# Hybrid encoder trunk: activations spread over the next products, the first pair's weight operands by way of DRAM, and a fixed TensorE order around the output projection

## The chip, the cores and the metric

The kernel runs on one core of a Trainium2 chip: TensorE (PE) multiplies, VectorE (DVE), ScalarE (ACT) and GpSimd (POOL) do the elementwise work, SyncE (SP) and the other engines' queues issue transfers (DMA) between device memory (DRAM) and the on-chip memory; products accumulate in banks of PSUM. The metric is the device time of one execution in microseconds, median of the runs.

## The reference

One layer of a Hymba-like encoder over two inputs, x_prompt (1, 256, 1024) and x_sample (1, 1024, 1024), all in float32, so 1280 tokens in all, ten tiles of 128:

```python
def encoder_layer(x, ...):
    h = rmsnorm(x, attn_norm_g)
    proj = h @ w_in
    a = mla_group(...)
    b = na_group(...)
    mix = jnp.concatenate([rmsnorm(a, mla_out_g), rmsnorm(b, na_out_g)], axis=-1)
    x = x + mix @ w_o
    h2 = rmsnorm(x, ffn_norm_g)
    x = x + (jax.nn.silu(h2 @ w_gate) * (h2 @ w_up)) @ w_down
    return x
```

and a last rmsnorm. `a` is latent attention, `b` neighbourhood attention, 512 columns each. D_MODEL is 1024, the FFN is 2816 wide (22 blocks of 128, taken as 11 pairs). The change touches what begins with `x + mix @ w_o` and ends ahead of `@ w_down`.

## The kernel before

**Split products.** Each float32 operand is split into a high part (a cast to fp32r, made on ACT or POOL) and a low part (the operand less its high part, made on DVE or POOL). A product is three matmuls, high by high, high by low, low by high (`mm3`, L108 to L112).

**Output projection.** The ten tiles t run one after the other. `mix_in` (L868) loads a tile of attention output `m`, squares it on ACT (L878), gets `rm`, the reciprocal root, on POOL (`rstd_of`, L89 and L91) and scales on POOL (L882). `mix_T` (L887) turns it by 8 transposes into `trm` and splits it (ACT L99, DVE L100) into `mT`. `out_proj` (L902) has 16 products of 128x512 in two banks `po`; DVE adds them to the residual `x` (L913). `ffn_in` (L918) squares x on ACT (L922), gets `rh` on POOL, scales on DVE (L925) to h2, turns it by 8 more transposes `trh` (L937), and evicts them with the gain (DVE L941, ACT L947) into X[k, j]: four blocks k of 256 features by three blocks j of 428 tokens (the last 424 used).

**Gate and up projections.** Each pair of feature blocks is multiplied by a fast bilinear scheme: 20 products of sums of weight blocks (weight operands `wr`) by sums of X (`S[n]`, n = 1 to 20), added up in PSUM chains and evicted into `C` (first use by ACT L1113, later ones added by DVE L1111). A product is 6 matmuls of 128x428 (`product`, L1097). For pair fp = 0, gate G and up U are multiplied together, 240 matmuls in the order `SEQ0`. After that come 20 phases of 120 matmuls in the order `SEQ`: for each pair 1 to 10 first gate (i = 0), then up (i = 1); the last phase has `SEQ0` again. The S operands are sums on DVE (`sums`, L965) and splits (`put_S`, ACT L958, DVE L959); some are made under the output projection, the rest under the first pair (`build_S`). Weight operands are sums on POOL (`sum_w`, L998), a cast on ACT (L990) and a low part on POOL or DVE (L992), in a ring of 3 slots at the first pair and 4 later. The raw weights come by SP, 1 MB for each phase.

**Activation.** `gate` is SiLU on ACT (L1129). `activate` (L1131) multiplies U by G in four blocks on DVE (L1132) and makes the sums which the down projection wants (L1138). Each result is stored to DRAM (`act_d`) by a DMA that ACT issues (`store`, L67):

```python
            if i == 1 and not last_one:
                if at == 10:
                    activate(G, C, "22", fp)
                elif at == 15:
                    activate(G, C, "12", fp)
```

The blocks "11" and "21" follow behind the up phase's last product, and fall in the next gate phase.

**Order.** SP's instructions run as written. On the other engines a scheduler sets the order when the program is built, from its own costs; `issue_after` holds a piece behind another instruction. Each engine then runs its instructions strictly in that order, and one that waits holds up all behind it.

Of the kernel before, what the change touches and what calls it, by code (L numbers as in the profile page):

```python
# [2 lines left out]

# [15 lines left out]
P = 128  # L19
# [20 lines left out]
def encoder_trunk(ctx: ExitStack, tc: tile.TileContext, x_tm, x_T, g_attn, w_c, w_v, w_qk,  # L40
# [794 lines left out]
    SE = rS.tile([P, 10 * 2 * XC], F32R, name="SE").rearrange("p (n s c t) -> p n s c t", n=5,  # L835
# [11 lines left out]
    rw, rt0, rm, rt1, rxm = r3 = [pool(nm) for nm in ("r3w", "r3t0", "r3m", "r3t1", "r3x")]  # L847
# [20 lines left out]
    def mix_in(t):  # L868
# [4 lines left out]
        mn = rm.tile([P, D], F32, name="m", bufs=3)  # L873
        ss = rm.tile([P, 2], F32, name="ssm", bufs=2)
        r = rm.tile([P, 2], F32, name="rm", bufs=2)
        for i in range(2):
            hs = slice(i * 512, (i + 1) * 512)
            nc.scalar.activation(mn[:, hs], mx[:, hs], AF.Square, accum_out=ss[:, i:i + 1])  # L878
        rstd_of(r, ss, 512)
        for i in range(2):  # L880
            hs = slice(i * 512, (i + 1) * 512)
            mixed[0] = nc.gpsimd.tensor_scalar(out=mn[:, hs], in0=mx[:, hs],  # L882
                                               scalar1=r[:, i:i + 1], scalar2=1.0,
                                               op0=ALU.mult, op1=ALU.mult).ins
        return mn

    def mix_T(t, mn):  # L887
        mT = (rt1 if t % 2 else rt0).tile([P, 2, KC, P], F32R, name=f"mT{t % 2}")
        for q in range(2):
# [4 lines left out]
            last_split[0] = split_ps(mT[:, 0, 4 * q:4 * q + 4], mT[:, 1, 4 * q:4 * q + 4], tr)  # L894
        return mT
# [6 lines left out]
    def out_proj(t, mT, x):  # L902
        added = []
        for hf in range(2):
            hs = slice(hf * 512, (hf + 1) * 512)
            ps = po.tile([P, 512], F32, name="po", bufs=2)
            with ExitStack() as es:
                if t == 0 and hf:
                    es.enter_context(tc.issue_after(last_os[0]))
                for kc in range(KC):  # L910
                    last = mm3(ps, mT[:, 0, kc], mT[:, 1, kc], wo[kc][:, 0, hs],
                               wo[kc][:, 1, hs], kc == 0, kc == KC - 1)
            added.append(nc.vector.tensor_add(out=x[:, hs], in0=ps, in1=x[:, hs]).ins)  # L913
        return last, added

    normed = [None]

    def ffn_in(t, x):  # L918
# [6 lines left out]
        done_ = [nc.vector.tensor_scalar(out=h2, in0=x, scalar1=r, scalar2=1.0, op0=ALU.mult,  # L925
                                         op1=ALU.mult).ins]
# [6 lines left out]
        for q in range(2):  # L933
            tr = po.tile([P, 4, P], F32, name="trm" if t >= NT - 2 and q else "trh", bufs=1)
            for i in range(4):
                kc = 4 * q + i
                nc.tensor.transpose(tr[:, i], h2[:, kc * P:(kc + 1) * P], ident)  # L937
            for j, to, of in cuts:
                if q == 0:
                    for k in range(2):  # L940
                        ev = nc.vector.tensor_mul(  # L941
                            out=X[k, j][:, :, to], in0=tr[:, 2 * k:2 * k + 2, of],
                            in1=gf[:, 2 * k:2 * k + 2].unsqueeze(2).to_broadcast(
                                [P, 2, of.stop - of.start]))
# [4 lines left out]
        return done_ + [ev.ins]  # L949

    def put_S(n, raw_, negate=False):
# [5 lines left out]
        else:  # L957
            nc.scalar.copy(out=h, in_=raw_)  # L958
            nc.vector.tensor_sub(out=l, in0=raw_, in1=h)  # L959

    ADD, SUB = ALU.add, ALU.subtract

    def sums(eng, cs, *steps):
        for o, a, op, b in steps:
            eng.tensor_tensor(out=X[o][:, :, cs], in0=X[a][:, :, cs], in1=X[b][:, :, cs], op=op)  # L965
# [7 lines left out]
    def put_(n, at):  # L973
# [6 lines left out]
              put_(17, (2, 1)), add_((3, 0), (3, 1), SUB, (3, 0)), add_("14", (2, 1), ADD, (1, 1)),  # L980
              add_((0, 1), (0, 1), SUB, (3, 0)), add_((1, 1), (1, 1), SUB, (3, 0)))

    LAST_SUMS = {16: (("16", (2, 1), ADD, (1, 2)),), 15: (((1, 0), (1, 2), SUB, (1, 0)),),
                 1: (((2, 0), (1, 2), SUB, (2, 0)), ((2, 0), (2, 0), SUB, (2, 2)),
                     ((2, 2), (2, 2), SUB, "16")),
                 20: (((1, 2), (3, 2), SUB, (1, 0)),),
                 12: (((3, 2), (2, 0), ADD, (3, 2)),), 19: (((3, 1), (2, 0), ADD, (3, 1)),)}
# [20 lines left out]
    cur = mix_T(0, mix_in(0))  # L1008
    load(gf, g_ffn)
    def B(k, i=slice(0, 2)):  # L1010
        return raw[:, i, k]

    LATER = {4: FIRST[0:4], 5: FIRST[4:], 7: SECOND[0:4], 8: SECOND[4:]}
    for t in range(NT):
        with ExitStack() as es:
            if t:
                es.enter_context(tc.issue_after(last_split[0]))
            nxt = mix_T(t + 1, mix_in(t + 1)) if t + 1 < NT else None
        if t == 6:
            for i in range(2):  # L1020
                load_raw(0, i)
            with tc.issue_after(mixed[0]):
                sum_w(tmp[0], B(2), SUB, B(6))
                cast_w(ring[0][:, 0], ring[0][:, 1], tmp[0])
        if t == 7:
            with tc.issue_after(mixed[0]):
                cast_w(ring[1][:, 0], ring[1][:, 1], B(4))
        x = load_x(t)
        last_mm, anchors = out_proj(t, cur, x)
        anchors = anchors + ffn_in(t, x)  # L1030
        for job, ins in zip(LATER.get(t, ()), anchors):
            with tc.issue_after(ins):
                job()
        cur = nxt
    for n in (16, 15, 1, 20, 19, 12):
        sums(dve, slice(0, 296), *LAST_SUMS[n])
    for p_ in reversed(r3):
        p_.release()
    po.release()
    pm.append(pool("pm1", space=PSUM, side="right"))  # L1040

    l4 = [pool("l4c"), pool("l4w"), pool("l4s")]
    lC, lw, ls = l4
    G, U = [lC.tile([P, 2, NTOK], F32, name="C", bufs=3) for _ in range(2)]
    ring.append(lw.tile([P, 2, 2, 256], F32R, name="wr2"))
    tmp += [lw.tile([P, 2, 256], F32, name=f"wt{n}") for n in (1, 2)]
    spare = lw.tile([P, 2, 2, 256], F32, name="wr3")
    tmp += [spare[:, n] for n in range(2)]
# [580 lines left out]
```

## Time and profile before

| what | us |
|---|---|
| runs | 1634.3, 1636.06, 1636.46 |
| median | 1636.06 |
| profiled execution | 1636.93 |
| its span | 1635.2 |
| mean granted TensorE clock | 0.993 |

The profile shows one execution. A row of the timeline has the start, the duration, engine, line, operation, out<-in, shapes and count; in brackets the idle time of the engine just before, and what ended it. A row of waits has the engine and tile that waited, on what, then total us, how many times, and the longest. Line numbers are those of the kernel before. A matmul of 428 columns has a row of 0.36 us, but one starts every 0.19 us, as they are pipelined.

### The profile page before, as it was taken

To read this page: it belongs to the slowest core of one execution; us is meant where nothing else is said; L and a number is where in the kernel's file an instruction comes from. 1 tells how busy PE (TensorE), PEld (TensorE's weight loads), DVE (VectorE), ACT (ScalarE), POOL (GpSimd) and SP (SyncE) were. 2 spreads that over 40 slices of the span, in tenths; PEclk is the share of its full clock that TensorE was granted. 3 is DMA by queue.
4 is the path that set the end of the run, shared out by engine and by line. 5 is a ranking of instruction groups with operands and counts; after the bars stand their busy time and mean duration, and the time that the engine had idled before them with its cause. 6 is when DMAs were issued, how large, how long until landed. Compare 5 with 4: busy or idle time off the path is not lost.

```text
span 1635.2 us, 23820 instructions
## 1 busy us (share of the span) xinstructions
PE 1569.2 (96%) x8560; PEld 1398.4 (86%) x8560; DVE 1032.9 (63%) x1624; ACT 774.5 (47%) x1576; POOL 747.0 (46%) x922
## 2 busy tenths in 40 slices
PE   8999999999999999999789999999999999999998
PEld 8888888998888888877588999999999987788886
DVE  5853044466777777334876766566766566876676
ACT  6523145465777778434344334334333443443334
POOL 4633135544211148223469787777787761010002
PEclk9999999999999999999899999999999999999999
DMA  8625022161100121234002322222222225943434
GB/s 287 200 74 154 21 52 61 37 223 48 29 22 24 39 100 40 97 116 178 29 29 106 108 83 82 87 74 108 108 83 78 91 107 213 334 145 97 155 102 153
DMA packets 111974, 170.45 MB, mean 104 GB/s; under 512 B 34288, under 2 KB 64752, under 8 KB 109040
## 3 DMA queue, kind: packets, MB, share of 16 engines
q1 hardware_dynamic: 69088, 119.77, 22.8%
q10 hardware_dynamic: 41952, 46.08, 8.2%
q0 software_dynamic: 816, 3.08, 0.5%
q8 instruction: 67, 1.10, 0.3%
q14 instruction: 51, 0.42, 0.1%
HBM read 118.44 MB, written 50.46 MB: 103 GB/s over the span
## 4 chain that ended last, share of the span: by engine, by line
PE 80%; DVE 11%; ACT 3%; issue 2%; DMA 2%; POOL 1%; SPq 0%; ACTq 0%; POOLq 0%; DVEq 0%
PE M L110 8%; PE M L111 8%; PE M L112 8%; PE d L110 5%; PE d L112 5%; PE d L111 5%; DVE C L1138 4%; PE o L788 4%; PE tp L778 4%; PE na_o L512 3%; PE pj L110 2%; PE pj L111 2%; PE pj L112 2%; PE po L110 2%; PE po L111 2%
## 5 line engine op out<-in xcount | busy, mean ns | idle before, releaser
L1111 DVE TENSOR_TENSOR C<-M,C 128x428 f32<-128x428 f32 (+1 forms) x242 | 143.1, 597 | 148.8 <-PE M L112 78.4
L992 POOL TENSOR_TENSOR wr<-wt,wr 128x512 fp32r<-128x512 f32 (+1 forms) x112 | 154.4, 1378 | 102.3 <-ACT wr L990 102.2
L110 PE MATMUL M<-s,wr 128*128 128x428 f32 x352 | 128.5, 366 | 17.6 <-ACT wr L990 10.3
L990 ACT CAST wr<-wt 128x512 fp32r<-128x512 f32 (+1 forms) x112 | 67.4, 602 | 154.1 <-PE M L111 126.6
L111 PE MATMUL M<-s,wr 128*128 128x428 f32 x352 | 127.4, 362 | 9.1 <-DVE s L959 9.1
L112 PE MATMUL M<-s,wr 128*128 128x428 f32 x352 | 126.8, 362 | 2.4 <-POOL wr L992 2.4
L100 DVE TENSOR_TENSOR PT<-tp,PT 128x512 fp32r<-128x512 f32 (+1 forms) x144 | 93.2, 658 | 34.1 <-ACT PT L99 32.8
L1113 ACT COPY C<-M 128x428 f32<-128x428 f32 (+1 forms) x132 | 66.3, 513 | 87.4 <-PE M L112 83.3
L990 ACT CAST wr<-wraw 128x512 fp32r<-128x512 f32 (+1 forms) x96 | 56.4, 596 | 83.0 <-PE M L111 50.5
L99 ACT CAST PT<-tp 128x512 fp32r<-128x512 f32 (+1 forms) x144 | 79.2, 568 | 33.9 <-PE tp L778 30.6
L110 PE MATMUL M<-x,wr 128*128 128x428 f32 x264 | 94.4, 358 | 0.9 <-DVE C L1111 0.6
L112 PE MATMUL M<-x,wr 128*128 128x428 f32 x264 | 93.6, 357 | 0.0
L770 DVE TENSOR_REDUCE mm<-S 128x1 f32<-128x1024 f32 (+1 forms) x80 | 84.9, 1061 | 13.5 <-PE S L112 11.9
L110 PE MATMUL d<-SE 128*128 128x512 f32 (+1 forms) x238 | 92.3, 388 | 0.6 <-DVE x L1411 0.6
L111 PE MATMUL d<-SE 128*128 128x512 f32 (+1 forms) x238 | 92.0, 387 | 0.0
L112 PE MATMUL d<-SE 128*128 128x512 f32 (+1 forms) x238 | 91.7, 387 | 0.0
L801 POOL TENSOR_TENSOR ob<-ob 128x128 f32<-128x128 f32 x40 | 18.6, 465 | 156.5 <-ACT ob L798 141.4
L110 PE MATMUL M<-SE,wr 128*128 128x428 f32 x220 | 80.2, 365 | 9.0 <-ACT C L1113 8.1
L110 PEld LDWEIGHTS M<-s,wr 128*128 128x128 f32 x352 | 67.3, 192 | 25.0 <-ACT wr L990 13.9
L772 ACT ACTIVATE ex<-S,mm 128x1024 f32<-128x1024 f32 (+1 forms) x80 | 79.7, 997 | 14.9 <-DVE mm L770 13.6
L1138 DVE TENSOR_TENSOR C<-C 128x640 f32<-128x640 f32 x55 | 86.2, 1599 | 0.3
L1145 ACT CAST SE<-as 128x640 fp32r<-128x640 f32 x58 | 42.2, 727 | 91.6 <-issue 59.3
(454 smaller groups left out, 4873.3 us busy)
## 6 DMA issues: line engine op xcount, KB each, us to landing
as<-act_d SPq DMA_DIRECT2D x73, 320.0 KB
act_d<-C ACTq DMA_DIRECT2D x70, 320.0 KB
wraw<-in_w_gate_dram SPq DMA_DIRECT2D x11, 1024.0 KB
wraw<-in_w_up_dram SPq DMA_DIRECT2D x11, 1024.0 KB
w<-in_w_down_dram SPq DMA_DIRECT2D x44, 256.0 KB
x<-in_x_tm_dram SPq DMA_DIRECT2D x20, 512.0 KB
cT_d<-stg ACTq DMA_DIRECT2D x20, 320.0 KB
xm_d<-x ACTq DMA_DIRECT2D x10, 512.0 KB
```

The costliest lines, as they stand in the source:

```text
L99: i = nc.scalar.copy(out=hi, in_=ps)
L100: nc.vector.tensor_sub(out=lo, in0=ps, in1=hi)
L110: nc.tensor.matmul(out, lhsT=sh, rhs=mh, start=first, stop=False, **kw)
L111: nc.tensor.matmul(out, lhsT=sh, rhs=ml, start=False, stop=False, **kw)
L112: return nc.tensor.matmul(out, lhsT=sl, rhs=mh, start=False, stop=last, **kw).ins
L770: nc.vector.reduce_max(out=nm[:, u:u + 1], in_=S, axis=AX.X, negate=True)
L772: nc.scalar.activation(ex, S, AF.Exp, bias=nm[:, u:u + 1], scale=1.0, accum_out=l[:, u:u + 1])
L990: i0 = nc.scalar.copy(out=hi, in_=raw_)
L992: i1 = (eng or nc.gpsimd).tensor_tensor(out=lo, in0=raw_, in1=hi, op=SUB)
L1111: nc.vector.tensor_add(out=o, in0=ps[:, 0:XN[j]], in1=o)
L1113: nc.scalar.copy(out=o, in_=ps[:, 0:XN[j]])
L1138: nc.vector.tensor_tensor(out=out, in0=src_[0], in1=src_[1], op=ACT_OP[n][1])
```

## The change

It has three parts.

1. `activate` becomes `act_step`, one multiplication or sum at a time. Tables (`STEPS`) say behind which product of the next phases each stands, and each is held behind the last eviction on DVE (`evicted`). The stores of the sums go out on SP (`load`) in place of ACT's queue. Of the last pair, whose stores already went out on POOL's queue, the steps follow single evictions.
2. The 18 weight operands of the first pair are made on POOL (high and low) during tiles 0 to 6 of the output projection, two or three a tile, in two slots; SP stores each to DRAM (`wop_d`) and loads it back into a ring of four slots just before its product. The raw weights for it are loaded at tiles 0, 1 and 2. The S sums of the third token block, which depend on the last tile, are divided: columns 0 to 168 on POOL under tile 9, the others on DVE in the first pair; S 14, 5 and 6 are made under tile 9. `SEQ0` is a new order, and the last phase has one of its own, `SEQL`.
3. From tile 1 to the end of the first pair TensorE's order is as written. The transposes of the next tile's `m` stand behind products 2 and 6 of a tile's 16, those of the last tile's h2 behind products 10 and 13. `mix_in` runs two tiles ahead. The last tile's h2 is turned among the first pair's products (behind its third product, both of gate and up, and behind the gate half of its fourth).

```diff
-    def activate(G, U, b, fp):
-        nc.vector.tensor_mul(out=block(U, b), in0=block(U, b), in1=block(G, b))
-        for n in AFTER[b]:
...
-            (store_p if fp == NF // 2 - 1 else store)(act_d[n][fp], out)
+    def act_step(G, U, fp, what):
+        if isinstance(what, tuple):
...
+            nc.vector.tensor_mul(out=U[:, f, cs], in0=U[:, f, cs], in1=G[:, f, cs])
...
+            (store_p if fp == NF // 2 - 1 else load)(act_d[what][fp], out)
...
+    STEPS = {(0, 0): ((0, 1), 3), (0, 1): (1,), (0, 2): (7,), (0, 4): (2,), (0, 8): (5,),
+             (0, 12): (6,), (1, 12): ("22", 4), (1, 16): ("12",), (1, 18): ((0, 0),),
+             (1, 19): ((0, 2),)}
...
+            with tc.issue_after(evicted[0]):
...
+                for what in steps_:
+                    act_step(*((G, U) if i else old), fp - (not i), what)
```

```diff
+    def early_operands():
+        b = [raw[:, :, k] for k in range(8)] + [tmp[0]]
+        for n, v, sums_ in ((13, 4, ()), (14, 5, ()), (1, 2, ()), (7, 0, ()), (8, 3, ()),
+                            (5, 1, ()), (12, 7, ()), (9, 8, ((8, 2, SUB, 6),)),
...
+            for o, x, op, y in sums_:
+                nc.gpsimd.tensor_tensor(out=b[o], in0=b[x], in1=b[y], op=op)
+            if len(kept) == 2:
+                load_r(*kept.pop(0))
+            w = ring[count[0] % 2]
...
+            nc.gpsimd.tensor_scalar(out=w[:, 0], in0=b[v], scalar1=1.0, scalar2=1.0,
+                                    op0=ALU.mult, op1=ALU.mult)
+            nc.gpsimd.tensor_tensor(out=w[:, 1], in0=b[v], in1=w[:, 0], op=SUB)
+            kept.append((wop_d[n], w))
+            yield
...
     for at in range(20):
-        if at + AHEAD0 < 20:
-            with tc.issue_after(normed[0]) if at else ExitStack():
-                w0.append(make(at + AHEAD0))
...
+        if at and at + 3 < 20:
+            load_r(ring[(at + 3) % 4], wop_d[SEQ0[at + 3][0]])
+        if at in (5, 7):
+            load_raw(1, at == 7)
+        if at in BUILD:
+            with tc.issue_after(evicted[0]):
+                build_S(BUILD[at])
```

```diff
+        if t == 1:
+            pe_order.enter_context(tc.manual_schedule(engines={mybir.EngineType.SP,
+                                                               mybir.EngineType.PE}))
+        if t + 2 < NT:
+            with tc.issue_after(last_split[0]):
+                coming = mix_in(t + 2)
+        x = load_x(0) if t == 0 else x_next
+        x_next = load_x(t + 1) if t + 1 < NT else None
+        for job in kept:
+            load_r(*job)
...
+        with tc.issue_after(mixed[0]):
+            for _ in range(2 if 1 < t < 6 else 1):
+                next(early, None)
...
+            between[1] = lambda: half_m(0)
+            between[5] = second_m
...
+            between[9 if t < 9 else 8] = first_h
+            between[12 if t < 9 else 11] = lambda half=last_half: half(1)
...
+        last_half = ffn_in(t, x)
+        with tc.issue_after(normed[0]):
+            next(early, None)
+            if t == 8:
+                third_2(gps, slice(0, 168))
```

How the instructions stand now. First POOL in the middle of the output projection, before: all that a tile has there, the two reciprocal roots and the scale of m (line numbers are each kernel's own).

```order
L89 TENSOR_SCALAR rh<-ssh 128x1
L91 TENSOR_TENSOR rh<-rh,mhalf 128x1
L89 TENSOR_SCALAR rm<-ssm 128x2
L91 TENSOR_TENSOR rm<-rm,mhalf 128x2
L882 TENSOR_SCALAR m<-m,rm 128x512 x2
```

POOL of the change, in a tile with three operands; `wr_` are the two slots, L1064 the sums of raw weights, L1069 and L1071 an operand's high and low part.

```order
L90 TENSOR_SCALAR rh<-ssh 128x1
L92 TENSOR_TENSOR rh<-rh,mhalf 128x1
L1064 TENSOR_TENSOR wraw<-wraw 128x2x256
L1069 TENSOR_SCALAR wr_8114<-wraw 128x512
L1071 TENSOR_TENSOR wr_8114<-wraw,wr_8114 128x512
L90 TENSOR_SCALAR rm<-ssm 128x2
L92 TENSOR_TENSOR rm<-rm,mhalf 128x2
L886 TENSOR_SCALAR m<-m,rm 128x512 x2
L1064 TENSOR_TENSOR wt_8115<-wt_8115,wraw 128x512
L1069 TENSOR_SCALAR wr_8113<-wt_8115 128x512
L1064 TENSOR_TENSOR wraw<-wraw 128x2x256
L1071 TENSOR_TENSOR wr_8113<-wt_8115,wr_8113 128x512
```

The operands have come in between the small operations on which the next tile waits.

DVE at the start of the first pair of the change, from the last tile's two additions to its scale (`s_` are S operands' low parts, L1235 and L1239 evictions of the pair's chains, L944 the scale of h2):

```order
L930 TENSOR_TENSOR x<-po,x 128x512 x2
L984 TENSOR_TENSOR s_9378<-st,s_9378 128x856
L1235 COPY C<-M_9397 128x428
L1235 COPY C<-M_9397 128x424
L984 TENSOR_TENSOR s_9381<-x_8104,s_9381 128x856
L1235 COPY C<-M_9406 128x428
L1235 COPY C<-M_9406 128x424
L984 TENSOR_TENSOR s_9384<-x_8101,s_9384 128x856
L1239 TENSOR_TENSOR C<-M_9416,C 128x424
L1239 TENSOR_TENSOR C<-M_9416,C 128x428
L944 TENSOR_SCALAR m<-x,rh 128x1024
```

There, before, the scale stood behind five x sums (`L965`), with no eviction ahead of it; now products run beside it, and their evictions stand in its queue.

ACT at the start of a gate phase, before (L67 are the stores of sums, L990 casts of weight operands, L1113 copies out of PSUM):

```order
L67 DMA act_d_108<-C 128x640
L990 CAST wr_8113<-wt_8115 128x512
L1113 COPY C<-M_10465 128x428
L67 DMA act_d_64<-C 128x640
L1113 COPY C<-M_10465 128x424
L67 DMA act_d_75<-C 128x640
L67 DMA act_d_119<-C 128x640
L990 CAST wr_8114<-wraw 128x512
```

DVE at the same place of the change (L1239 evictions, L1264 multiplications of U by G in pieces, L1272 sums, L1020 the low part of the operand that plays the part of the last row above):

```order
L1239 TENSOR_TENSOR C<-M_11108,C 128x424
L1264 TENSOR_TENSOR C<-C 128x428
L1272 TENSOR_TENSOR C<-C 128x640
L1264 TENSOR_TENSOR C<-C 128x424
L1264 TENSOR_TENSOR C<-C 128x428
L1272 TENSOR_TENSOR C<-C 128x640
L1239 TENSOR_TENSOR C<-M_11262,C 128x424
L1272 TENSOR_TENSOR C<-C 128x640
L1020 TENSOR_TENSOR wr_8114<-wraw,wr_8114 128x512
```

ACT has no store there any more, and the sums on DVE stand singly, with evictions between; the operand's low part stands behind three of them.

More of the change, by code (lines that the diff above doesn't have):

```diff
@@ L900, in load_x, with out_proj @@
         return x
[L902 to L904 removed]
+    def out_proj(t, mT, x, between):
+        ps = {}
+        order = [(hf, kc) for hf in range(2) for kc in range(KC)]
+        if t == NT - 1:
+            order = [(hf, kc) for kc in (4, 0, 1, 5, 2, 3, 6, 7) for hf in range(2)]
+        count_ = [0, 0]
+        for at, (hf, kc) in enumerate(order):
             hs = slice(hf * 512, (hf + 1) * 512)
[L906 removed]
+            if hf not in ps:
+                ps[hf] = po.tile([P, 512], F32, name="po", bufs=2)
             with ExitStack() as es:
@@ L909, in out_proj @@
                     es.enter_context(tc.issue_after(last_os[0]))
[L910 to L916, printed above, removed]
+                last = mm3(ps[hf], mT[:, 0, kc], mT[:, 1, kc], wo[kc][:, 0, hs],
+                           wo[kc][:, 1, hs], count_[hf] == 0, count_[hf] == KC - 1)
+            count_[hf] += 1
+            if count_[hf] == KC:
+                added[0] = nc.vector.tensor_add(out=x[:, hs], in0=ps[hf], in1=x[:, hs]).ins
+            if at in between:
+                between[at]()
+        return last
+    normed, added = [None], [None]
     def ffn_in(t, x):
@@ L1007, in encoder_trunk @@
         load_wo(n, pl, nm)
-    cur = mix_T(0, mix_in(0))
+    junk = [None, pm[0].tile([P, 512], F32, name="M0", bufs=4)]
+    cur, half = mix_T(0, mix_in(0))
+    half(0)
+    half(1)
     load(gf, g_ffn)
+    ahead = mix_in(1)
     def B(k, i=slice(0, 2)):
         return raw[:, i, k]
[L1013 to L1031, printed above, removed]
+    wop_d = {n: tc.dram_tile([P, 2, 2, 256], F32R, name=f"wop_d{n}") for n in
+             (13, 14, 1, 12, 7, 8, 5, 9, 17, 16, 3, 15, 19, 20, 2, 4, 18, 10)}
```

321 lines of the change are left out of this document (203 added, 118 removed), and 14 rows, old and new, of tables (SEQ0, SEQL).

## The prediction

> **What bounds the kernel now.** I read the head of the page first, then the waits of TensorE, then the stages that the change touches. The profiled execution took 1636.93 us, 1635.2 of it span; the median of the runs is 1636.06.
>
> ```profile
> PE 1569.2 (96%) x8560; PEld 1398.4 (86%) x8560; DVE 1032.9 (63%) x1624; ACT 774.5 (47%) x1576; POOL 747.0 (46%) x922
> PE 80%; DVE 11%; ACT 3%; issue 2%; DMA 2%; POOL 1%; SPq 0%; ACTq 0%; POOLq 0%; DVEq 0%
> L1111 DVE TENSOR_TENSOR C<-M,C 128x428 f32<-128x428 f32 (+1 forms) x242 | 143.1, 597 | 148.8 <-PE M L112 78.4
> L1138 DVE TENSOR_TENSOR C<-C 128x640 f32<-128x640 f32 x55 | 86.2, 1599 | 0.3
> ```
>
> TensorE is the bound, with 80% of the chain that ended last. The matmuls stay the same in number and shape, so only TensorE's idle time, and time at a reduced clock, can go. From the first gate/up product (794.4) on, its idle time has these releasers up to 1364:
>
> ```profile
> PE M L110 <- ACT wr L990: 10.6, 11, 1.2
> PE M L111 <- DVE s L959: 9.1, 1, 9.1
> PE M L110 <- ACT C L1113: 8.1, 11, 1.1
> PE M L110 <- DVE C L1111: 6.7, 4, 3.7
> PE M L112 <- POOL wr L992: 2.4, 1, 2.4
> PE M L110 <- ACT s L958: 2.0, 1, 2.0
> ```
>
> The stages in which they lie (columns: window, its length, then busy time and count of PE, PEld, DVE, ACT, POOL, then granted clock, DMA share and GB/s) are output projection; first pair; gate phase of pair 1; all phases up to the last; last phase; the rest:
>
> ```profile
> 660.70:794.40 133.70, 131.99 (x657) 107.53 (x656) 56.08 (x90) 50.46 (x128) 33.54 (x63) 1.00 0.35 123
> 794.40:860.70 66.30, 49.48 (x234) 45.65 (x233) 55.08 (x57) 31.50 (x52) 46.91 (x32) 0.87 0.10 40
> 860.70:893.20 32.50, 29.01 (x138) 26.31 (x137) 25.71 (x28) 13.45 (x20) 30.92 (x23) 0.95 0.28 104
> 893.20:1335.10 441.90, 425.75 (x2162) 404.45 (x2161) 290.95 (x334) 170.71 (x289) 345.88 (x270) 1.00 0.26 92
> 1335.10:1361.80 26.70, 24.15 (x121) 21.98 (x120) 15.93 (x28) 15.16 (x32) 12.94 (x17) 1.00 0.12 47
> 1361.80:1635.20 273.40, 265.44 (x1172) 217.40 (x1170) 191.94 (x286) 107.88 (x183) 22.54 (x32) 0.99 0.53 177
> ```
>
> For a floor I take an up phase, which has 120 matmuls and hardly a stall. Three starts, of a gate phase, its up phase and the next gate phase:
>
> ```profile
> 916.57 0.36 PE L110 MATMUL M<-s,wr 128*128 128x428 f32 x1
> 942.30 0.36 PE L110 MATMUL M<-s,wr 128*128 128x428 f32 x1
> 965.64 0.36 PE L110 MATMUL M<-s,wr 128*128 128x428 f32 x1
> ```
>
> 965.64 − 942.30 = 23.34, or 0.1945 us a matmul. The gate phase ahead of it took 25.73. So the 18 phases in 441.9 us lose 441.9 − 18 × 23.34 = **21.8**; the last phase loses 26.7 − 23.34 = **3.4**. The first two windows hold 360 matmuls (70.0) and 8 transposes (0.9 by 0.11 apiece) in 98.8 us: **27.9** lost. The output projection is idle for 133.70 − 131.99 = 1.7: nothing to be had. All idle time that the change aims at is 53.1.
>
> **Part 1, activations singly, stores off ACT's queue.** A gate phase loses its 2.4 us in two places:
>
> ```profile
> 924.44 0.47 PE L110 MATMUL M<-SE,wr 128*128 128x428 f32 x1 [0.69 <-ACT C L1113]
> 928.21 0.47 PE L110 MATMUL M<-s,wr 128*128 128x428 f32 x1 [1.15 <-ACT wr L990]
> ```
>
> ACT is late because it holds the stores of the sums in its own order, and each store waits until DVE, working through a block of six, has made its sum. One such block, in the next gate phase:
>
> ```profile
> 969.38 6.85 DVE L1138 TENSOR_TENSOR C<-C 128x640 f32<-128x640 f32 x4
> 974.42 2.16 ACTq L67 DMA_DIRECT2D act_d<-C  x2
> 976.62 0.62 ACT L990 CAST wr<-wraw 128x512 fp32r<-128x512 f32 x1 [3.14 <-DVE C L1138]
> 977.34 0.69 DVE L992 TENSOR_TENSOR wr<-wraw,wr 128x512 fp32r<-128x512 f32 x1 [0.61 <-ACT wr L990]
> ```
>
> With the 70 stores on SP, ACT's cast comes early and its stall goes. What is late next is the same operand's low half (operands 8 and 12) on DVE: ahead of it now stand, from about 0.5 us into the phase, two evictions (2 × 0.6), three multiplications of 424 to 428 columns (1.6 × 428/640 = 1.07 each), three steps of 640 columns (1.6 each by L1138) and itself (0.7): 9.9 in all, ready at 10.4. TensorE takes it after 56 matmuls, at 56 × 0.1945 = 10.9. A margin of 0.5 is not safe, as the steps took 1.71 each in the block above: 0 to 0.8 lost per pair. I take 0.36 × 9 = 3.2, and 1.0 for the small losses of up phases: 4.2 of 21.8 stay, **−17.6**. The bounds are −21 (none stays) and 0 (rival B). SP's 70 stores stand in written order among its loads; SP issues a raw load of 1 MB only every 23 us, so I price that at nothing; without this cover a late raw load would stop POOL's sums.
>
> **Part 2, first operands made early; part 3, the fixed order.** The first pair's stalls, and DVE and POOL beside them:
>
> ```profile
> 805.92 1.08 PE L110 MATMUL M<-s,wr 128*128 128x428 f32 x2 [2.03 <-ACT s L958]
> 816.10 0.72 PE L111 MATMUL M<-s,wr 128*128 128x428 f32 x1 [9.10 <-DVE s L959]
> 843.38 0.62 PE L110 MATMUL M<-s,wr 128*128 128x428 f32 x1 [3.72 <-DVE C L1111]
> 844.16 0.56 PE L112 MATMUL M<-s,wr 128*128 128x428 f32 x1
> 844.52 0.56 PE L110 MATMUL M<-s,wr 128*128 128x428 f32 x1
> 805.42 5.74 DVE L965 TENSOR_TENSOR x<-x,x 128x264 f32<-128x264 f32 x4
> 809.42 1.45 POOL L992 TENSOR_TENSOR wr<-wraw,wr 128x512 fp32r<-128x512 f32 x1
> 815.97 0.42 DVE L965 TENSOR_TENSOR x<-x,x 128x264 f32<-128x264 f32 x1
> 816.31 1.04 DVE L959 TENSOR_TENSOR s<-st,s 128x856 fp32r<-128x856 f32 x1
> ```
>
> The 9.1 us wait is for S operands whose sums crept: 1.44 each beside a working POOL, 0.42 as soon as it stopped. After the wait of 3.72 matmuls stand 0.36 apart instead of 0.19: the clock was halved, the 0.87 of the window. Now 18 operands come back from DRAM by SP; POOL has none to make in the first half of this pair, and S 14, 5 and 6 are ready first. What is left by my count:
> - the transposes of the last tile, in the fixed order behind three products: its scale on DVE stands behind two x sums (2 × 0.68), three lows (3 × 1.04), evictions (4 to 8 × 0.6) and itself 0.75, ready at 8.6, against TensorE at 3 × 12 × 0.1945 = 7.0: 1.6;
> - the last S operands: DVE has 26 evictions (15.6), 15 lows (15.6), sums of 5.3 + 3.1 and 2.9 of the last tile, 42.5 undisturbed, against 18 × 12 × 0.1945 + 0.9 = 42.9 on TensorE. Balanced, and POOL works beside it from the middle on, since the next pair's raw weights are loaded at products 5 and 7: 2 to 3;
> - part of the clock loss, about 1, and the gate phase of pair 1, where old sums still stand among evictions: 2.5.
>
> That is 8 of the 27.9: **−19.9**. The ends are 3 (only the first and some clock) and 18 (rival D).
>
> What is added lies under the output projection, POOL above all. Its prices, and DVE's of a tile:
>
> ```profile
> 756.49 1.30 POOL L992 TENSOR_TENSOR wr<-wt,wr 128x512 fp32r<-128x512 f32 x1 [1.54 <-ACT wr L990]
> 757.87 1.30 POOL L998 TENSOR_TENSOR wt<-wt,wraw 128x512 f32<-128x512 f32 x1
> 771.81 0.19 POOL L89 TENSOR_SCALAR rh<-ssh 128x1 f32<-128x1 f32 x1 [7.38 <-ACT m L922]
> 774.67 0.70 POOL L91 TENSOR_TENSOR rm<-rm,mhalf 128x2 f32<-128x2 f32 x1
> 775.47 1.37 POOL L882 TENSOR_SCALAR m<-m,rm 128x512 f32<-128x512 f32 x2
> 826.41 2.11 POOL L992 TENSOR_TENSOR wr<-wt,wr 128x512 fp32r<-128x512 f32 x1
> ```
>
> Tiles 2 to 5 make three operands each, tile 4 with four sums. A high half is the same operation as L882, 0.69; a low or a sum 1.30. Tile 4: 4 × 1.3 + 3 × (0.69 + 1.3) + 3.0 for rh, rm and m = 14.2, against 133.70 × 640/657/10 = 13.0 on TensorE; tiles 3 and 5 about 12.9. POOL falls 1.2 us behind and catches up in tile 6. The tile's h2 is needed after ten products of the next tile (30 × 0.2335 plus transposes, 7.9 us), and by the chain sum, square, rh, scale is ready after 4.0: 3.9 of slack. A ring of two slots adds waits for the stores of operands, of which the page shows nothing nearer than POOL's other waits; from below nothing, from above 2 a tile. I cost the output projection at **0**, with the 1.7 that it loses now; ends −1.7 and +18 (the 27 lows and sums of tiles 2 to 6 at 2.11, so 0.81 more each, 21.9, less the slack of 3.9).
>
> **Last phase:** its own steps follow evictions and the down operands are split over it: **−1.0** of 3.4, between 0 and −3.
>
> Sum: −17.6 − 19.9 + 0 − 1.0 = −38.5, so 1636.93 − 38.5 = 1598.4 by the profiled execution; the median stands 0.87 below it: **1597.6**.
>
> **Rivals.**
> - B, the stall moves from ACT to DVE. If the steps run at 1.9 beside POOL (345.88 of 441.9 us busy in that stage), the low half comes at 11.2 to 12, and the evictions behind it free banks late: up to the old 2.4 in each of nine gate phases, 21.8 lost instead of 4.2. Against it: DVE's busy time is 66% there. Time 1615. Chance 0.09.
> - C, POOL paces the output projection. If DVE's and POOL's operations prolong each other there as they did at 805, seven tiles lose about 1: 1604.6; at the upper end, 1615.6. Against it: DVE is busy for only 56.08 of 133.70. Chance 0.12. The Trainium skill, "SBUF — State Buffer", section "Who interferes with whom", calls this an exclusive lock on the shared port pair, for a DVE instruction with two SBUF inputs; by that rule, x sums and scales here would block, while evictions from PSUM would not. The trace agrees at 805.42 and 815.97 (1.44 and 0.42).
> - D, the first pair is bound by DVE. If its lows take 1.38 and the sums as much more (POOL started early), 42.5 becomes 51 to 53, 8 to 10 more: 1607. Chance 0.08.
> - E, slower. POOL waits for a ring slot until an operand's DRAM store has landed, and the store waits in SP's order behind the next tile's loads; rh stands behind it, so each of nine tiles waits. To lose the 38.5, every tile would have to cost 4.3 more, so POOL's tile be 3.9 + 4.3 over TensorE's 13, or 21 us, against 14.2 worked out. At 6 a tile: 1652. Chance 0.03.
> - F, the waits that go uncover equal ones (a sum that isn't there because a store holds up SP's loads in their turn): within 3 of before. Chance 0.02.
>
> **How the numbers follow.** The forecast has 0.66, with its own range of 1588 to 1606 (terms' ends: 21 and 25 saved below, half of each above). The range for 8 in 10 takes in the likelier halves of C and D and ends just short of B: **1586 to 1614**. Below 0.2% (3.3 us, what a measurement of this kernel tells from no change) I put F; E is slower, with half of a chance for milder forms: faster 0.94, same 0.02, slower 0.04.
>
> **What would show it.** Right: gate phases of 23.4 to 23.9 from start to start, no ACT store in them; the first pair at 53 or less with a clock near 1.00 and no wait above 2; the output projection's length unchanged; POOL near 95 us busy in it (18 highs and lows, 20 sums and 7 for x sums on top of its own 28). Wrong: waits for `wr` lows on DVE at the eleventh product (B), transposes of h2 that wait for POOL's rh (C, E), waits for S lows late in the first pair (D). Wrong as a whole it would be if the two 20 us terms weren't both there.

## The result and the profile after

| | before | changed |
|---|---|---|
| median of the runs, us | 1636.26 (1634.3 to 1636.9, 4 runs) | 1598.49 (1596.72 to 1600.68, 4 runs) |
| ratio | 1 | 0.9772, 95% interval 0.9755 to 0.9789 |
| profiled execution's span, us | 1635.2 | 1597.2 |

The changed kernel is 2.3% faster. 1597.6 was predicted. The sum came out, but its terms did not: two savings are larger than forecast, and a stage that was put at no cost took about as much back, as the table of stages shows. The head of the page after:

```profile
PE 1559.9 (98%) x8560; PEld 1395.4 (87%) x8560; DVE 1015.4 (64%) x1656; ACT 761.1 (48%) x1552; POOL 766.1 (48%) x961
PE 84%; DVE 4%; POOL 4%; DMA 3%; ACT 2%; issue 2%; SPq 0%; ACTq 0%; POOLq 0%; DVEq 0%
```

DVE's share of the chain that ended last fell from 11% to 4%, while POOL's rose from 1% to 4%. The stages of the changed kernel (columns as in the prediction's table), from the first matmul of the output projection on: output projection; first pair with the gate phase of pair 1; the 18 phases; the last phase; the rest:

```profile
661.92:802.96 141.04, 132.98 (x650) 107.86 (x651) 64.61 (x100) 50.64 (x125) 92.97 (x120) 0.99 0.56 195
802.96:878.58 75.62, 72.54 (x370) 67.86 (x369) 67.30 (x94) 31.79 (x49) 34.13 (x29) 1.00 0.53 182
878.58:1298.61 420.03, 420.03 (x2161) 405.17 (x2160) 275.35 (x344) 170.76 (x289) 343.38 (x271) 1.00 0.29 97
1298.61:1324.67 26.06, 24.71 (x122) 21.90 (x121) 17.25 (x27) 14.68 (x32) 18.58 (x23) 1.00 0.27 90
1324.67:1597.20 272.53, 265.31 (x1171) 217.30 (x1169) 193.13 (x287) 107.64 (x183) 23.13 (x33) 0.99 0.52 175
```

The same edges before are 661.35 (first matmul of the output projection), 794.38, 893.15, 1335.06 and 1361.96 (first matmul of the down projection).

| stage | before | changed | difference | predicted |
|---|---|---|---|---|
| output projection | 133.03 | 141.04 | +8.0 | 0 |
| first pair and first gate phase | 98.77 | 75.62 | −23.2 | −19.9 |
| 18 phases | 441.91 | 420.03 | −21.9 | −17.6 |
| last phase | 26.90 | 26.06 | −0.8 | −1.0 |

With the start 0.6 later and the rest 0.7 shorter that makes 38.0, the difference of the spans. In the 18 phases TensorE is now at its floor (18 × 23.34 = 420.1). In the output projection it waits more than before. All of its waits there and from there to the last phase, in the changed kernel:

```profile
PE trh L957 <- DVE x L961: 6.1, 3, 2.6
PE trh L957 <- DVE m L944: 1.8, 3, 0.8
PE M L111 <- DVE C L1239: 2.1, 2, 1.4
PE trh L957 <- DVE m L944: 0.7, 1, 0.7
```

The first two rows, 7.9 us, are the output projection's: the transposes of h2 wait for DVE, most for the eviction (L961) of the half turned before. How that comes about shows in one tile. TensorE's two waits, then DVE, then the end of ACT's square, which `rh` needs, then POOL:

```profile
739.94 0.63 PE L957 MATMUL trh<-ident,m 128*128 128x128 f32 x4 [0.80 <-DVE m L944]
745.24 0.63 PE L957 MATMUL trh<-ident,m 128*128 128x128 f32 x4 [2.58 <-DVE x L961]
...
738.01 1.78 DVE L944 TENSOR_SCALAR m<-x,rh 128x1024 f32<-128x1024 f32 x1 [3.54 <-POOL rh L92]
739.72 0.68 DVE L901 TENSOR_TENSOR mT<-trm,mT 128x512 fp32r<-128x512 f32 x1
740.32 2.00 DVE L984 TENSOR_TENSOR SE<-x,SE 128x428 fp32r<-128x428 f32 x2
742.24 0.68 DVE L930 TENSOR_TENSOR x<-po,x 128x512 f32<-128x512 f32 x1
742.84 1.58 DVE L992 TENSOR_TENSOR x<-x,x 128x428 f32<-128x428 f32 x2
744.35 0.74 DVE L961 TENSOR_TENSOR x<-trh,gf 128x256 f32<-128x256 f32 x2
...
733.07 0.19 ACT L941 ACTIVATION_READ_ACCUMULATOR m<-x 128x1 f32 x1
...
735.19 1.28 POOL L1064 TENSOR_TENSOR wraw<-wraw,wt 128x512 f32<-128x512 f32 x1
736.57 0.19 POOL L90 TENSOR_SCALAR rh<-ssh 128x1 f32<-128x1 f32 x1
736.84 0.62 POOL L1069 TENSOR_SCALAR wr<-wraw 128x512 fp32r<-128x512 f32 x1
737.42 0.56 POOL L92 TENSOR_TENSOR rh<-rh,mhalf 128x1 f32<-128x1 f32 x1
```

Three things add up. The small rh operations stand behind operand work on POOL: the square was ready at 733.3, rh at 738.0. DVE's scale takes 1.78 us beside POOL; with POOL idle it takes 0.74 (see "no early POOL work" below). Then DVE has S work (L984, L992) in its queue ahead of the eviction; the bank `trh` has one buffer, so the second half of the transposes waits for all of it.

### The profile page after: what moved, and what is told of

The parts are those of the page before. It is cut to its first block, busy times and chain, and to the rows that moved or that the text cites. A ratio compares the mean times of both kernels' runs of the same rounds, so it can differ in the third digit from the quotient of the medians.

```text
span 1597.2 us, 23983 instructions
## 1 busy us (share of the span) xinstructions
PE 1559.9 (98%) x8560; PEld 1395.4 (87%) x8560; DVE 1015.4 (64%) x1656; ACT 761.1 (48%) x1552; POOL 766.1 (48%) x961
## 4 chain that ended last, share of the span: by engine, by line
PE 84%; DVE 4%; POOL 4%; DMA 3%; ACT 2%; issue 2%; SPq 0%; ACTq 0%; POOLq 0%; DVEq 0%
PE M L112 10%; PE M L113 10%; PE M L111 10%; PE d L111 6%; PE d L113 6%; PE d L112 6%; PE o L789 4%; PE tp L779 4%; PE na_o L513 3%; PE pj L111 2%; PE pj L112 2%; PE pj L113 2%; PE S L111 2%; PE S L113 2%; PE S L112 2%
## 5 line engine op out<-in xcount | busy, mean ns | idle before, releaser
L1239 DVE TENSOR_TENSOR C<-M,C 128x428 f32<-128x428 f32 (+1 forms) x263 | 150.9, 594 | 145.5 <-PE M L113 74.8
L1020 POOL TENSOR_TENSOR wr<-wt,wr 128x512 fp32r<-128x512 f32 (+1 forms) x106 | 149.3, 1409 | 68.3 <-ACT wr L1018 68.1
L1018 ACT CAST wr<-wt 128x512 fp32r<-128x512 f32 (+1 forms) x106 | 63.2, 599 | 132.9 <-PE M L112 123.7
L111 PE MATMUL M<-s,wr 128*128 128x428 f32 x352 | 125.7, 357 | 0.1
L112 PE MATMUL M<-s,wr 128*128 128x428 f32 x352 | 125.4, 356 | 0.1
L113 PE MATMUL M<-s,wr 128*128 128x428 f32 x352 | 125.2, 357 | 0.0
L112 PE MATMUL d<-SE 128*128 128x512 f32 (+1 forms) x238 | 91.8, 387 | 0.0
L111 PE MATMUL d<-SE 128*128 128x512 f32 (+1 forms) x238 | 89.6, 388 | 0.0
L113 PE MATMUL d<-SE 128*128 128x512 f32 (+1 forms) x238 | 89.6, 387 | 0.0
L779 PE MATMUL tp<-ident,ex 128*128 128x128 f32 x544 | 79.2, 274 | 2.4 <-DVE PT L101 1.3
L789 PE MATMUL o<-PT,v 128*128 128x256 f32 x544 | 80.6, 287 | 0.8 <-ACT PT L100 0.8
L90 POOL TENSOR_SCALAR ry<-ssy 128x1 f32<-128x1 f32 x5 | 4.1, 817 | 157.6 <-ACT yo L1571 157.5
```

The source lines that it names most:

```text
L111: nc.tensor.matmul(out, lhsT=sh, rhs=mh, start=first, stop=False, **kw)
L112: nc.tensor.matmul(out, lhsT=sh, rhs=ml, start=False, stop=False, **kw)
L113: return nc.tensor.matmul(out, lhsT=sl, rhs=mh, start=False, stop=last, **kw).ins
L779: nc.tensor.transpose(tp[:, j], ex[:, kt * P:(kt + 1) * P], ident)
L789: nc.tensor.matmul(oT, lhsT=vv, rhs=pt[s][g][:, j], start=kt == 0 and s == 0, stop=kt == nkt - 1 and s == 1)
L1020: i1 = (eng or nc.gpsimd).tensor_tensor(out=lo, in0=raw_, in1=hi, op=SUB)
```

## The experiments

Each is the changed kernel with one edit, timed beside runs of the kernel before; "two a tile", "operands sooner", "sooner, order free" and "scale on ACT" hold the edit of "jobs behind trh" as well, and the last two that of "operands sooner" too. The stages are read from the same three matmuls of one profile each (first of the output projection, of the first pair, of the down projection). In the kernels whose edit doesn't touch the output projection, that stage took 138.6 to 141.0, so single differences of 2 us in it tell little.

| kernel | median, us | ratio to before (95%) | output projection | gate and up |
|---|---|---|---|---|
| changed | 1598.49 | 0.9772 (0.9755 to 0.9789) | 141.04 | 521.71 |
| changed, run again | 1597.79 | 0.9761 (0.9747 to 0.9775) | 140.02 | 521.74 |
| stores on ACT | 1604.78 | 0.9806 (0.9791 to 0.9821) | 140.82 | 529.46 |
| blocks, stores on SP | 1610.38 | 0.9836 (0.9821 to 0.9851) | 138.56 | 534.51 |
| no early POOL work | 1588.88 | 0.9704 (0.9689 to 0.9718) | 130.33 | 521.75 |
| no early operands | 1610.37 | 0.9840 (0.9825 to 0.9856) | 131.73 | 541.45 |
| jobs behind trh | 1595.22 | 0.9748 (0.9732 to 0.9764) | 136.60 | 522.07 |
| order free | 1594.03 | 0.9743 (0.9726 to 0.9759) | 656.27 for both | |
| third block on DVE | 1600.93 | 0.9785 (0.9771 to 0.9800) | 139.18 | 523.49 |
| two a tile | 1605.91 | 0.9816 (0.9801 to 0.9830) | 147.05 | 522.60 |
| operands sooner | 1592.84 | 0.9731 (0.9717 to 0.9745) | 134.54 | 521.85 |
| sooner, order free | 1593.04 | 0.9732 (0.9718 to 0.9745) | 656.44 for both | |
| scale on ACT | 1593.77 | 0.9736 (0.9722 to 0.9749) | 133.92 | 520.94 |

With the free order, products of the first pair start ahead of the last tile, so that the two stages are one (662.75 in the changed kernel).

**Part 1, taken in two.** First the stores back on ACT's queue:

```diff
-            (store_p if fp == NF // 2 - 1 else load)(act_d[what][fp], out)
+            (store_p if fp == NF // 2 - 1 else store)(act_d[what][fp], out)
```

> The changed kernel with one thing undone: the 70 stores of the activation's sums go out on ACT's queue again; the single steps stay where the change put them. If the gain of the 18 later phases comes from ACT being free of waiting stores, gate phases lose again about what they lost before, 2 us each, and the whole is 15 to 20 us slower than the changed kernel. If the gain comes from the steps being single and spread, so that a store finds its sum done when ACT reaches it, the whole is within 3 us of the changed kernel.

Gate and up take 7.8 us more than in the changed kernel, between the two expectations. ACT holds a store, and the copy behind it, until the sum is made. Its rows of the waits over the 18 phases, and TensorE's:

```profile
ACT C L1241 <- DVE C L1272: 55.1, 18, 4.9
...
PE M L111 <- ACT C L1241: 2.5, 9, 0.3
```

Each of the nine gate phases loses some 0.9 (the listed 0.3, and matmuls around it that start up to 0.2 late). Then the steps in blocks again, with the stores on SP:

```diff
+            if i == 1 and not last_one and at in (10, 15):
+                activate("22" if at == 10 else "12", fp)
...
+        elif not last_one:
+            activate("11", fp)
+            activate("21", fp)
```

> The other half undone: for pairs 1 to 9 the multiplications and sums stand in blocks again, behind the 11th and 16th product and behind the last product of the up phase, while their stores go out on SP. If the stall moves from ACT to DVE (the rival B of the prediction), the low half of the 11th product's operand stands behind two multiplications and several sums: ready near 11.3 us after the phase's start against the 10.9 at which TensorE takes it, and evictions behind the block come late too: 0.7 to 1.5 a gate phase, 6 to 14 us slower than the changed kernel. If taking the stores off ACT was enough, within 2 us of it.

12.8 us more in gate and up: the stall does move from ACT to DVE (rival B), but by another of the two paths that it named. A gate phase, DVE's rows, then TensorE's wait:

```profile
904.15 6.86 DVE L1272 TENSOR_TENSOR C<-C 128x640 f32<-128x640 f32 x4
910.93 0.59 DVE L1239 TENSOR_TENSOR C<-M,C 128x424 f32<-128x424 f32 x1
911.44 0.70 DVE L1020 TENSOR_TENSOR wr<-wraw,wr 128x512 fp32r<-128x512 f32 x1
...
911.57 0.46 PE L111 MATMUL M<-x,wr 128*128 128x428 f32 x1 [1.24 <-DVE C L1239]
```

It is the eviction behind the block, whose bank a chain wants, that TensorE waits for. In the 18 phases alone, undoing the two halves costs 8.2 and 13.1, together 21.3 of the 21.9 that those phases gained: each is needed, and their costs add.

**Part 2: what the early operands cost and bring.** First POOL's work on all but the first two of them left out under the output projection, the traffic to and from DRAM kept (so the first pair multiplies by values that were not computed):

```diff
-            for o, x, op, y in sums_:
-                nc.gpsimd.tensor_tensor(out=b[o], in0=b[x], in1=b[y], op=op)
...
+            if count[0] < 3:
+                nc.gpsimd.tensor_scalar(out=w[:, 0], in0=b[v], scalar1=1.0, scalar2=1.0,
...
```

> In the output projection POOL's work on the first pair's operands is left out but for the first two operands (16 operands' high and low parts and 20 sums are not computed, the stores and loads by way of DRAM stay), so the results differ. If POOL's work is what costs the output projection its 9.3 us (through rh, and through DVE's operations that take longer beside it), about 8 us faster than the changed kernel, with DVE's scale at 0.74 us a tile in place of 1.77. If it is SP's stores and loads, or the place of DVE's jobs alone, within 2 us of it.

The output projection takes 130.33, 10.7 us less, and this window and DVE's scale in the middle of it read:

```profile
660.90:791.20 130.30, 130.11 (x650) 107.03 (x651) 57.45 (x100) 50.33 (x125) 42.66 (x75) 1.00 0.61 211
...
730.72 0.74 DVE L944 TENSOR_SCALAR m<-x,rh 128x1024 f32<-128x1024 f32 x1
```

TensorE has no idle time left (130.11 of 130.30). So POOL's work is what brings the whole loss of that stage; the 18 stores and the loads cost nothing there. It is even 2.7 shorter than before the change. Then the operands made while the first pair runs, in three slots, by ACT and POOL, as before the change:

```diff
-            load_r(ring[(at + 3) % 4], wop_d[SEQ0[at + 3][0]])
...
+        if at + 2 < 20:
+            make(at + 2)
```

> The changed kernel without early operands: no POOL work for them under the output projection, no stores to and loads from DRAM; the first pair's operands are cast on ACT and their low parts made on POOL while it runs, in three slots, as before the change, but in the changed kernel's product order and with its written TensorE order. The output projection should get its 9 to 11 us back. If the first pair's gain is that of the early operands, it falls behind POOL and DVE again (40 POOL operations of 1.3 to 2.1, 52 to 84 us, against 47.6 on TensorE, and DVE's S work prolonged beside them): first pair 10 to 30 us longer, the whole 0 to 20 slower than the changed kernel. If the gain is that of the order and of S 14, 5 and 6 being early, the first pair stays within 3 us and the whole is 6 to 11 us faster.

The output projection gets 9.3 us back, gate and up lose 19.7: early operands are worth 10 to 12 us in the whole. The first pair's window of that kernel and its two longest waits:

```profile
794.90:866.00 71.10, 55.49 (x248) 49.80 (x247) 60.20 (x72) 31.49 (x52) 57.22 (x42) 0.88 0.10 38
...
805.62 0.72 PE L113 MATMUL M<-SE,wr 128*128 128x428 f32 x1 [5.53 <-POOL wr L1020]
829.02 0.73 PE L111 MATMUL M<-SE,wr 128*128 128x428 f32 x1 [5.59 <-ACT wr L1018]
```

POOL is busy for 57.22 of 71.10, DVE for 60.20, and the clock falls to 0.88, much as before the change (0.87). From its first matmul to that of the gate phase behind it, the first pair takes 71.3 here, 49.2 in the changed kernel and 70.2 before: without early operands the product order, S 14, 5 and 6 and the written order gain nothing in it. What is left of this stage's gain, 23.2 − 19.7 = 3.5, lies in the gate phase of pair 1, which takes 23.9 here, 26.4 in the changed kernel and 28.6 before.

The third token block's sums on DVE:

```diff
-            if t == 8:
-                third_2(gps, slice(0, 168))
...
-            third_2(dve, slice(168, XC))
+            third_2(dve, FULL)
```

> The sums of the third token block all on DVE in the first pair (428 columns in place of 260; none on POOL under the last tile). The prediction took DVE for all but full in the first pair (42.5 us of work against 42.9). If so, the 8 x 0.35 = 2.8 us more of it show on TensorE, 2 to 4 us slower than the changed kernel, with waits for S operands. If DVE has slack there, within 1 us of it.

Gate and up take 1.8 more, the output projection 1.9 less, and the ratio's interval overlaps the changed kernel's: not settled by the times. The profile has one new wait in the first pair, of 2.1 us for an eviction on DVE, none for S operands.

**The output projection's loss.** DVE's jobs moved behind the eviction:

```diff
-                behind_now(ev[0], jobs[2])
-                if t == 8:
-                    behind_now(ev[0], jobs[3])
+                for job in jobs:
+                    behind_now(ev[0], job)
```

with the two other places (behind `last_low` and `added`) taken out.

> The S sums and low parts that DVE makes under tiles 5, 6 and 8 stand behind the eviction of the tile's first half of turned h2 (trh), instead of partly ahead of it; nothing else moves. If TensorE's waits for the second half (2.6, 2.5 and 1.0 us) come from what stands ahead of that eviction in DVE's queue, they go: 5 to 7 us faster than the changed kernel with the reduced clock behind them. If they come from rh being late on POOL, only 1 us or less.

4.4 us off that stage by the profiles, 3.3 by the medians (the two ratios' intervals just overlap, so the waits decide). DVE in the tile that was shown:

```profile
735.82 1.78 DVE L944 TENSOR_SCALAR m<-x,rh 128x1024 f32<-128x1024 f32 x1 [3.36 <-POOL rh L92]
737.51 0.68 DVE L901 TENSOR_TENSOR mT<-trm,mT 128x512 fp32r<-128x512 f32 x1
738.12 0.68 DVE L930 TENSOR_TENSOR x<-po,x 128x512 f32<-128x512 f32 x1
738.71 0.74 DVE L961 TENSOR_TENSOR x<-trh,gf 128x256 f32<-128x256 f32 x2
739.37 2.19 DVE L984 TENSOR_TENSOR SE<-x,SE 128x428 fp32r<-128x428 f32 x2
```

The eviction starts 2.9 us after the scale, not 6.3 as before this edit, and TensorE's waits for it fall from 6.1 to 0.2. Those for the scale rise from 1.8 to 2.4: with that wait gone, rh is what comes last. Next, two operands a tile over tiles 0 to 8 (`range(1)` in place of `range(2 if 1 < t < 6 else 1)`), jobs behind trh kept:

> DVE's jobs behind trh as in the last run, and besides two operands a tile on POOL over tiles 0 to 8 instead of three over tiles 2 to 5. The longest wait left there was 2.15 us for DVE's scale, which waits for rh on POOL. If POOL's load of a tile (14 us with four sums against 13 on TensorE) is what makes rh late, the output projection loses 3 to 5 us less than with the jobs behind trh alone, 1590 to 1593 in all. If rh is late at any load because long operations stand ahead of it in the queue, or if the last tile's rh is now late behind POOL's later operands, no gain.

Slower, and for neither of the reasons named. POOL's last operand, SP's queue, and TensorE's first product of the pair:

```profile
802.34 1.26 POOL L1071 TENSOR_TENSOR wr<-wraw,wr 128x512 fp32r<-128x512 f32 x1
...
803.62 0.32 SPq L77 DMA_DIRECT2D wop_d<-wr  x1
804.05 11.23 SPq L77 DMA_DIRECT2D wr<-wop_d  x6
...
808.36 0.70 PE L111 MATMUL M<-SE,wr 128*128 128x428 f32 x1 [11.35 <-DMA wr<-wop_d]
```

The last operand's store waits in SP's order for POOL, and the loads for the first products stand behind it, though their operands were stored long before. Without that 11.35 the stage would be at about 135.7 (an estimate). So the operands were moved the other way:

```diff
-            for _ in range(2 if 1 < t < 6 else 1):
+            for _ in range(2 if 0 < t < 4 else 1):
```

> The jobs behind trh, and POOL's 18 operands moved to earlier tiles: three a tile over tiles 1 to 3 and two over tiles 4 to 6, so that the tile with four sums no longer has three operands and the last operand is stored well ahead of the loads for the first products (the run with two a tile lost 11.4 us there to SP's order). If POOL's load in tiles 4 to 6 is what makes rh late, the 2.15 us wait for DVE's scale goes and the output projection loses 2 to 3 us less than with the jobs behind trh alone: about 1592. If it only moves the late rh to tiles 2 and 3, no gain over 1595.

1592.84: 2.7% under the kernel before, and 5 us under the changed kernel run again beside it (1597.79). With the two below it, from which it can't be told apart, it is the fastest of the kernels that compute everything. The output projection is at 134.54, 2.1 less than with the jobs behind trh alone. The late rh has moved with the operands: three waits for the scale, 3.4 us in all against 2.4, so waits for it are not what this edit saved. None is over 1.4 now, where one was 2.15; behind that one the granted clock was 0.50 from 753.1 to 756.5, which costs 1.7, and here there is no such stretch in the stage.

TensorE's order left to the scheduler, first in the changed kernel, then with the operands sooner and the jobs behind trh:

```diff
-            pe_order.enter_context(tc.manual_schedule(engines={mybir.EngineType.SP,
-                                                               mybir.EngineType.PE}))
+            pass
```

> The changed kernel with TensorE's order left to the scheduler from tile 1 to the end of the first pair; all else as changed. If the first pair's gain rests on the written order (products while the last tile's h2 is turned), the wait for the last tile comes back, about 5 to 10 us slower than the changed kernel. If it rests on operands and S sums being ready early, within 3 us of the changed kernel; and if the written order costs the output projection its waits for turned h2 (the second half stands three products behind the first), that stage gets shorter by a few us.

> The same with TensorE's order left to the scheduler. If the written order costs only by its waits for turned h2, which are gone already, the same time as the run before within 2 us. If the scheduler's order also lets products of the first pair start under the last tiles, 2 to 4 us less: 1588 to 1590.

Alone it gains 6.5 us over both stages by the profiles (662.75 to 656.27), 4.5 by the medians: there is no wait for the eviction (L961) left in its profile, and no stretch at half clock in these stages. With the two other edits it adds nothing (656.39 with the written order, 656.44 with the free one): the waits for L961 are gone already, and what it saves in others goes to one stretch of 3.4 us at half clock, behind a wait of 2.06. So the written order is not what the first pair's gain rests on. As their yardstick:

> The changed kernel once more, on the chip and beside the runs of these two, as their yardstick: 1598 to 1599.

Last, the scale of h2 on ACT:

```diff
-        scaled[0] = nc.vector.tensor_scalar(out=h2, in0=x, scalar1=r, scalar2=1.0, op0=ALU.mult,
-                                            op1=ALU.mult).ins
+        scaled[0] = nc.scalar.activation(h2, x, AF.Copy, scale=r).ins
```

> The operands made sooner and the jobs behind trh as two runs ago, and the scale of h2 moved from DVE to ACT (an activation with a factor for each row). TensorE's waits there were 4.0 us in all, all for that scale: rh is late on POOL, and the scale itself takes 1.77 us beside POOL in place of 0.74. If the part of the stall that is contention between DVE and POOL is what is left, ACT's scale takes about 1.1 us wherever POOL is busy, and four waits lose 0.7 each: 2 to 3 us faster, about 1590. If rh being late is all that matters, within 1 us of 1593; if ACT's queue (evictions of trh, squares) holds the scale up, slower by 2 to 5 us.

The time is the same within what the runs tell (the ratios' intervals overlap almost wholly). The scale itself behaves as expected. The line in the changed kernel on DVE, and in this one on ACT (min, median, max in ns):

```profile
L944 DVE TENSOR_SCALAR m<-x,rh x10: 734/1068/1780, 679.7 to 809.9; 128x1024 f32<-128x1024 f32 x10
...
L944 ACT ACTIVATE m<-x,rh x10: 1135/1153/1157, 680.6 to 800.9; 128x1024 f32<-128x1024 f32 x10
```

Beside the same POOL work, ACT's takes the same each time, and TensorE's waits for it fall to 1.9 from 4.0 (the first pair's counted in). One for DVE's addition to x comes in their place, 1.3. The two stages together are 1.5 shorter (654.86 against 656.39); this profile loses 1.8 in the down projection, most of it in and around a wait of 1.0 for a weight's low part, which the profile of "operands sooner" has not. Whether the edit causes that wait is not shown.

## Why the prediction was right, point by point

- **The bound and the floor.** Right: TensorE, and 23.34 a phase; the 18 phases now take 18 of them.
- **The signs that it named.** Gate phases take 23.3 from start to start, the first pair 49.2 with the clock at 1.00 and no wait above 0.7, POOL is busy for 92.97 in the output projection: as forecast or better. The output projection's length, which was to stay, did not.
- **Part 1, −17.6 predicted, −21.9 measured.** The mechanism was right, and the two halves undone show it. The mis-sized step is "0.36 × 9 = 3.2, and 1.0 for the small losses of up phases": none of it stayed. The low half of the operand was put at 10.4 after the phase's start, and there it is. In the changed kernel a gate phase starts, and DVE makes that part, at:

```profile
901.94 0.36 PE L111 MATMUL M<-s,wr 128*128 128x428 f32 x1
...
911.10 1.22 DVE L1020 TENSOR_TENSOR wr<-wraw,wr 128x512 fp32r<-128x512 f32 x1
```

  so it ends 10.4 after, 0.5 ahead of need. That the time agrees is in part luck: the low half took 1.22 where 0.7 was put, the sums ahead of it 1.25 to 1.47 each where 1.6 was put. The margin called not safe held in every phase.
- **First pair, 8 predicted to stay of 27.9, 4.7 stayed.** That it rests on the early operands is shown (19.7 back without them). "The last S operands ... 2 to 3" was the wrong part: there is no wait for an S operand in the changed kernel. The wait for the last tile was 0.7, not 1.6, and no clock was lost. The first gate phase lost more than its 2.5: 26.4 against 23.34, so 3.1, of which 2.1 are listed waits.
- **Output projection, 0 predicted, +8.0 measured.** This step failed: "3.9 of slack" was worked out for the chain square, rh, scale alone. It left out that the second half of the transposes waits on DVE's eviction of the first, in a single bank, behind S work which POOL prolongs. Waits went from 1.7 to 7.9, and the clock, 0.88 in 754 to 768, took about as much as is left (14 × 0.12 = 1.7). Rival C had the place, at 7, and one part of the cause: without POOL's work the loss is gone, but with all of that work kept, 3.3 to 4.4 of it goes with the place of DVE's jobs alone, which no rival named. The savings forecast for the first pair and the 18 phases were too small, by 3.3 and 4.3, about what this term was too hopeful; that the sum came out at 1598 is luck to that extent.
- **The stores on SP** cost TensorE no listed wait where the change put them. With two operands a tile the same queue cost 11.4, the mechanism of rival E at another place: a store that waits, and loads behind it.
- **What the change could have had.** All 53 us were aimed at; 45.9 came, and 8.0 were given back to POOL's load under the output projection, of which the run with operands sooner has 6.5 again.

## What to carry to other kernels

Idle time on an engine is not free room: what is put there delays the small operations that others wait for, and prolongs a neighbour's. Look for each such operation's place in that queue, and for single buffers whose release stands behind other work. A fault in an ordered queue (stores held by ACT, evictions behind a block, loads behind a late store) is cured by the place in the order, and moving the holder to another queue helps only if nothing urgent stands behind it there. A sum that comes out right can hide errors of both signs; compare it by stage.

## What the runs showed of the hardware

- DVE's scale, one input of 128x1024, took 0.74 us with POOL idle and up to 1.78 beside it; two-input sums of 128x428 took 0.59 with POOL idle and 0.59 to 1.07 beside it; ACT's scale took 1.14 to 1.16 in all ten tiles. The Trainium skill, "SBUF — State Buffer", section "Who interferes with whom", says that a `tensor_scalar` in a two-port mode takes the port pair that DVE shares with GpSimd, and that ACT never waits; the runs agree. The prediction weighed that lock for the sums and the scale, but put its price only in a rival.
- What a wait costs in clock depends on where it lies. In all profiles the granted clock changes in steps of 3.41 us (the stretches at half clock last 3.41, 10.24 or 13.65, but for the one that the program's end cuts off). In the changed kernel a wait of 2.58 us, ended at 745.24, lies across two steps, and the clock stays at 1.00; one of 2.51, ended at 760.76, lies whole in one, and the next step has 0.50. The four steps (columns as above):

```profile
740.33:743.74 3.41, 2.33 (x12) 1.58 (x9) 3.41 (x5) 0.09 (x1) 3.24 (x4) 1.00 0.83 280
743.74:747.15 3.41, 1.91 (x11) 1.68 (x12) 2.38 (x6) 1.25 (x5) 3.22 (x4) 1.00 0.45 181
757.40:760.81 3.41, 0.90 (x5) 0.44 (x4) 3.22 (x6) 0.82 (x1) 3.06 (x4) 1.00 0.90 357
760.81:764.22 3.41, 3.41 (x11) 2.83 (x12) 1.35 (x2) 1.22 (x5) 3.32 (x4) 0.50 0.43 145
```

  TensorE is idle for 1.1 and 1.5 in the first two and for 2.5 in the third. In all 14 profiles, from 30 us on, every step at full clock with 1.9 us or more of such idle time was followed by one at half clock, and none with 1.7 or less was; of the six between (1.74 to 1.85), one was. By these figures two waits of 1.4 in different steps cost 2.8, and one of 2.1 in a single step costs its 2.1 and 1.7 more.
